# Order and array quarters of the 64x64 products of a chunked recurrence, and the halves of its output bank

## The chip, the cores and the metric

The kernel runs on one core of one Trainium2 chip. The metric is the device time of the whole program in microseconds; 3 runs gave 843.79, 843.86 and 844.13, median 843.86 us. The profile shown is of a further execution, which took 844.05 us.

A core has a matrix engine (TensorE, PE in the profile, its weight loads listed as PEld), a vector engine (DVE), a scalar engine (ACT), GpSimd (POOL) and SyncE (SP), which here issues the loads of the weights. TensorE reads SBUF and writes PSUM; a matmul with 64 contraction rows and 64 output columns uses one quarter of the 128x128 array: its rows are set by the SBUF partitions of its operands (0 to 63 or 64 to 127), its columns by the PSUM partitions of its output. A quarter is called diagonal here when both are the same half, off-diagonal when they are not.

## The reference

One layer of a hybrid decoder on 512 tokens of 1024 channels, in float32: a norm, one input projection, two mixers (sparse attention and RWKV-7), a gated merge with an output projection, and a gated MLP. The change is in the RWKV-7 mixer, whose scan over tokens is, for each of 8 heads with a 64x64 state:

```python
def step(state, inp):
    r_t, w_t, k_t, v_t, a_t, b_t = inp
    sa = jnp.einsum('bhij,bhj->bhi', state, a_t)
    state = state * w_t[:, :, None, :] + sa[..., None] * b_t[:, :, None, :] + v_t[..., None] * k_t[:, :, None, :]
    return state, jnp.einsum('bhij,bhj->bhi', state, r_t)
...
_, y = lax.scan(step, state0, xs)
```

`y` is then normed per head, gated and projected.

## The kernel before

The scan is done in 8 chunks of 64 tokens (`C = 64`, `NCH = 8`). What a chunk needs of its own tokens alone is made beforehand and lies in SBUF: `AR` (decayed a and r vectors), `AB` (masked 64x64 products of a and r with b and k, the inverse of a triangular matrix among them), `BKT` (b and k transposed) and `UV`, of which one half holds the values v and the other half is filled in by the loop. Heads go in 4 pairs p with r = 0 or 1 within the pair; r decides the half of the partitions.

The loop over chunks c (line 935) has, in this order on TensorE, which is given its instructions as the program has them there (`tc.manual_schedule`, line 930):

- X (lines 937 to 941): the state `M0` times a, 8 products of 64x64 added to what `x_own` (lines 922 to 927) left in the same PSUM bank for this chunk. X's products have operands and output in the same half, `x_own`'s read the other half than they write.
- Y's first part (lines 942 to 944): `M0` times r, 8 products into a second bank, operands and output in the same half. In chunk 0 there is no state, and both are left out.
- DVE copies X to `Xs` (line 946); then a piece of other work, see below.
- U (lines 948 to 951): the inverse times `Xs`, 8 products. ACT copies one half of it into `UV` (line 952), DVE the other (line 953). Behind U on TensorE follows `x_own(c + 1)` (line 956), which opens the next chunk's X in another bank; then another piece of other work.
- the state update (lines 959 to 970): `BKT` times `UV` into the bank `Mp`, 8 products of 128 rows and 64 columns, and two operations on DVE that make the next state `M1`. The last chunk has none.
- Y's second part (lines 971 to 974): the r part of `AB` times `UV`, 8 products of 128 rows; two ACT copies take Y to `Ys` (lines 977, 978). Every second chunk `group_norm` norms 128 tokens and gates them (line 854).

X, U and the bank `gg` of `group_norm` share two PSUM banks (`pb()`), Y, `Mp` and others two more (`pa()`).

The other work comes from the generator `fill_chain` (line 880), one step at each `next(fill)`: dense products of the normed input with weight tiles of 128 columns (`dense_fm_g`, line 402: 16 matmuls with a tile's high part, with a pause after 12 of them, and 8 with its low part) and, in the first chunks, the first layer of the compression MLP (`compress`, line 786), which reads its weights as they were loaded. Weights pass through `wload` (line 262: SP issues a load of 512 KB into one of 3 buffers `raw`), and `wsplit_` (line 279: ACT writes the high part `whi`, DVE the rest `wlo`, two buffers each). A buffer `raw` is free again when the split, or TensorE's last product with it, is done. Between the compression's weights k and v and the next dense tile, loads are issued in that order: k, v, tile.

DVE, ACT and SP run what a scheduler put in order; each runs its queue in order.

Of the kernel before, what the change touches and what calls it, by code (L numbers as in the profile page):

```python
# [23 lines left out]
DH = 64  # L24
H = 8
NH2 = H // 2
C = 64
NCH = S // C
# [52 lines left out]
def hybrid_block(ctx: ExitStack, tc: tile.TileContext, A: dict, out: bass.AP):  # L81
# [25 lines left out]
    def bank(tag, bufs, shape=(128, 512)):  # L107
        return ps.tile(list(shape), F32, name="ps_" + tag, tag=tag, bufs=bufs)

    def mmb():  # L110
        return bank("mm", 4)

    def pa():
        return bank("a", 2)

    def pb():
        return bank("b", 2)

    def mm(o, l, r, start, stop):
        te.matmul(o, lhsT=l, rhs=r, start=start, stop=stop)  # L120

    def act(o, i, f=AF.Copy, **kw):
        sc.activation(o, i, f, **kw)  # L123

    def tt(o, a, b, op):
        v.tensor_tensor(o, a, b, op=op)  # L126

    def ts(o, a, s1, s2, op0=ALU.mult, op1=ALU.add):
        if s2 is None:
            v.tensor_scalar(o, a, s1, None, op0=op0)  # L130
        else:
            v.tensor_scalar(o, a, s1, s2, op0=op0, op1=op1)
# [44 lines left out]
    def rstd(ap, n, eps=1e-6, tag=""):  # L177
        p, w = ap.shape
        m, y = (cp.tile([128, 32], F32, name=k, tag=k + tag, bufs=2)[0:p, 0:w] for k in ("rs_m", "rs_y"))
        ts(m, ap, 1.0 / n, eps)  # L180
        ts(ap.bitcast(I32), m.bitcast(I32), -0.5, float(0x5f3759df))
        for i in range(3):
            tt(y, ap, ap, ALU.mult)
            stt(y, y, -0.5, m, ALU.mult, ALU.mult)
            stt(ap, y, 1.5, ap, ALU.add, ALU.mult)
# [209 lines left out]
    def run(g):  # L395
        while True:
            try:
                next(g)
            except StopIteration as e:
                return e.value  # L400
# [23 lines left out]
    AR = mp.tile([128, NH2, NCH, 2, C], F32, name="AR", tag="AR")  # L424

    AB = abp.tile([128, NCH, NH2, 2, 128], F32, name="AB")
    BKT = rp.tile([128, NCH, NH2, 2, DH], F32, name="BKT")
    UV = rp.tile([128, NCH, NH2, 2, DH], F32, name="UV")
# [193 lines left out]
    for g in range(2):  # L622
        for b in range(2):
            r = 64 * g + 32 * b
# [107 lines left out]
    for b in (1, 0):  # L732
        for g in range(2):
            r = 64 * g + 32 * b
# [119 lines left out]
    def group_norm(c0, Ys):  # L854
        n1 = tp.tile([128, H], F32, name="n1", tag="n1", bufs=2)
        bc = n1[:, :, None].to_broadcast([128, H, DH])
        v.tensor_reduce(n1, Ys, axis=AX.X, op=ALU.add)
        ts(n1, n1, -1.0 / DH, None)
        tt(Ys, Ys, bc, ALU.add)
        sq = tp.tile([128, H, DH], F32, name="sq", tag="o", bufs=2)  # L860
        act(sq, Ys, AF.Square)
        v.tensor_reduce(n1, sq, axis=AX.X, op=ALU.add)
        rstd(n1, DH, 64e-5, "g")
        tt(Ys, Ys, bc, ALU.mult)
        yield
        qs = slice(C * c0, C * c0 + 128)
        pt = pa()
        gg = pb()
        o = tp.tile([128, NH2, 128], F32, name="o", tag="o", bufs=2)
        for p in range(NH2):  # L870
            ps_ = slice(128 * p, 128 * p + 128)
            te.transpose(pt[:, ps_], Ys[:, 2 * p:2 * p + 2].rearrange("p h d -> p (h d)"), ident)
            mm(gg[:, ps_], g2[:, ps_], sg[:, qs], True, True)
        for p in range(NH2):
            act(o[:, p], pt[:, 128 * p:128 * p + 128], AF.Identity, scale=col("rwkv_ln_g", p),
                bias=col("rwkv_ln_b", p))
        tt(o, o, BO[:, :, qs], ALU.add)
        tt(BO[:, :, qs], o, gg.rearrange("p (a t) -> p a t", a=NH2), ALU.mult)
# [26 lines left out]
    def bias_rows(a):  # L905
        o = 127 - 16 * a
        nc.sync.dma_start(BT[16 * a:16 * a + 16, :, 256:512],
                          vd[:, 0:16 * 384].rearrange("h (i m) -> i h m", m=384)[:, :, o:o + 256])

    def bias_compressed():  # L910
        nc.gpsimd.memset(BC.rearrange("p j g e n -> p (j g e) n")[:, :, 31:56], NEG)
        for j in range(2):
            src = BT.rearrange("p (g j e) n -> p j g e n", g=2, j=2)[:, j]
            v.tensor_copy(BC[:, j, :, :, 0:15], src[:, :, :, 256:257].to_broadcast([128, 2, 2, 15]))
            v.tensor_copy(BC[:, j, :, :, 15:31], src[:, :, :, 271:512:16])
# [3 lines left out]
    def hsl(r, n=64):  # L919
        return slice(64 * r, 64 * r + n)  # L920

    def x_own(c, X):
        for p in range(NH2):
            for r in range(2):
                o = hsl(1 - r)
                mm(X[hsl(r), 64 * p:64 * p + 64], AB[o, c, p, r, 0:64], UV[o, c, p, r, :], p == 0,
                   c == 0 and p == NH2 - 1)


    with tc.manual_schedule(engines={mybir.EngineType.PE}):  # L930
        M0 = Ys = gn = None
        X = pb()
        x_own(0, X)
        next(fill, None)
        for c in range(NCH):
            Y = pa()
            if M0 is not None:
                for p in range(NH2):
                    for r in range(2):
                        mm(X[hsl(r), 64 * p:64 * p + 64], AR[hsl(r), p, c, 0, :], M0[hsl(r), p, :], False,  # L940
                           p == NH2 - 1)
                for p in range(NH2):
                    for r in range(2):
                        mm(Y[hsl(r), 64 * p:64 * p + 64], AR[hsl(r), p, c, 1, :], M0[hsl(r), p, :], p == 0, False)
            Xs = tp.tile([128, NH2, DH], F32, name="Xs", tag="Xs", bufs=2)
            v.tensor_copy(Xs, X[:, 0:256].rearrange("p (a d) -> p a d", d=DH))
            next(fill, None)
            U = pb()
            for p in range(NH2):
                for r in range(2):  # L950
                    mm(U[hsl(r), 64 * p:64 * p + 64], AB[hsl(r), c, p, r, 0:64], Xs[hsl(r), p], True, True)
            act(UV[0:64, c, :, 0, :], U[0:64, 0:256].rearrange("p (a d) -> p a d", d=DH))
            v.tensor_copy(UV[64:128, c, :, 1, :], U[64:128, 0:256].rearrange("p (a d) -> p a d", d=DH))
            if c < NCH - 1:
                X = pb()
                x_own(c + 1, X)
            next(fill, None)
            if c < NCH - 1:
                Mp = pa()
                for p in range(NH2):  # L960
                    for r in range(2):
                        mm(Mp[hsl(r), 64 * p:64 * p + 64], BKT[:, c, p, r, :], UV[:, c, p, r, :], True, True)
                M1 = tp.tile([128, NH2, DH], F32, name="M", tag="M", bufs=2)
                mpv = Mp[:, 0:256].rearrange("p (a d) -> p a d", d=DH)
                pc = PC[:, :, c:c + 1].to_broadcast([128, NH2, DH])
                if M0 is None:
                    tt(M1, mpv, pc, ALU.mult)
                else:
                    tt(M1, M0, mpv, ALU.add)
                    tt(M1, M1, pc, ALU.mult)  # L970
            for p in range(NH2):
                for r in range(2):
                    mm(Y[hsl(r), 64 * p:64 * p + 64], AB[:, c, p, r, 64:128], UV[:, c, p, r, :],
                       M0 is None and p == 0, p == NH2 - 1)
            if c % 2 == 0:
                Ys = tp.tile([128, H, DH], F32, name="Ys", tag="Ys", bufs=2)
            for r in range(2):
                act(Ys[hsl(c % 2), r::2, :], Y[hsl(r), 0:256].rearrange("p (h d) -> p h d", d=DH))
            if c % 2 == 1:
                gn = group_norm(c - 1, Ys)  # L980
                if c < NCH - 1:
                    next(gn)
            M0 = M1
            if 4 <= c < 6:
                for a in range(4 * c - 16, 4 * c - 12):
                    bias_rows(a)
            if c == NCH - 2:
                bias_compressed()
            if c == NCH - 1:
                for h0 in range(0, H, 4):  # L990
                    act(BT[:, h0:h0 + 4, 0:256], BT[:, h0:h0 + 4, 256:257].to_broadcast([128, 4, 256]))
            next(fill, None)
            if gn is not None and c % 2 == 0:
                run(gn)
                gn = None
# [294 lines left out]
    with tc.manual_schedule(engines=KTS):  # L1290
        for t in range(NT):
            qs = slice(128 * t, 128 * t + 128)
            p = mmb()
# [88 lines left out]
```

## Time and profile before

| | |
|---|---|
| median of the runs | 843.86 us |
| profiled execution | 844.05 us, span 842.3 us |
| TensorE busy | 829.1 us of the span |
| DVE, ACT, POOL busy | 514.0, 405.9, 52.4 us |
| stretch of the recurrence | from 180 to 285 us of the span |

The granted TensorE clock is 1.000 over the span. A row of the timeline has the start in us from the span's beginning, the time in us, engine, source line, operation, what is written and read, the shape and how many instructions were merged into the row; in brackets the idle time before it and what ended that. Line 120 is the helper `mm`, 123 `act`, 126 `tt`, 135 `stt`; which work a row is, is told by the tiles.

### The profile page before, as it was taken

To read this page: it belongs to the slowest core of one execution; us is meant where nothing else is said; L and a number is where in the kernel's file an instruction comes from. 1 tells how busy PE (TensorE), PEld (TensorE's weight loads), DVE (VectorE), ACT (ScalarE), POOL (GpSimd) and SP (SyncE) were. 2 spreads that over 40 slices of the span, in tenths; PEclk is the share of its full clock that TensorE was granted. 3 is DMA by queue.
4 is the path that set the end of the run, shared out by engine and by line. 5 is a ranking of instruction groups with operands and counts; after the bars stand their busy time and mean duration, and the time that the engine had idled before them with its cause. 6 is when DMAs were issued, how large, how long until landed. Compare 5 with 4: busy or idle time off the path is not lost.

```text
span 842.3 us, 12845 instructions
## 1 busy us (share of the span) xinstructions
PE 829.1 (98%) x5097; PEld 674.3 (80%) x5097; DVE 514.0 (61%) x998; ACT 405.9 (48%) x784; POOL 52.4 (6%) x69
## 2 busy tenths in 40 slices
PE   7999999999999999999999999999999999999998
PEld 6777778887787886777788988888888888888886
DVE  5477779963556678888675576666556666322222
ACT  6766655452545677677344454444444444221210
POOL 6200020140000110111000000000000000000000
PEclk9999999999999999999999999999999999999999
DMA  7432222335461320010167033333333332223421
GB/s 228 115 82 68 75 75 76 92 104 156 126 126 51 88 63 13 22 31 26 51 204 234 0 99 90 90 97 100 100 100 100 96 90 93 98 100 113 138 75 51
DMA packets 109104, 78.73 MB, mean 93 GB/s; under 512 B 3869, under 2 KB 97748, under 8 KB 109044
## 3 DMA queue, kind: packets, MB, share of 16 engines
q1 hardware_dynamic: 106512, 73.51, 30.0%
q0 software_dynamic: 1472, 1.86, 1.0%
q10 hardware_dynamic: 1060, 2.55, 1.0%
q8 instruction: 40, 0.66, 0.3%
q14 instruction: 20, 0.16, 0.1%
HBM read 74.56 MB, written 2.29 MB: 91 GB/s over the span
## 4 chain that ended last, share of the span: by engine, by line
PE 53%; DVE 0%; DVEq 0%; issue 0%
PE ps_mm L120 52%; PE ps_b L203 0%; PE ps_a L203 0%; PE ps_a L120 0%; PE ps_b L1186 0%; PE ps_mm L1186 0%; DVE x L126 0%; DVEq L1378 0%; PE ps_a L1138 0%
## 5 line engine op out<-in xcount | busy, mean ns | idle before, releaser
L296 DVE TENSOR_TENSOR wlo<-raw,whi 128x1024 fp32r<-128x1024 f32 (+1 forms) x111 | 131.5, 1186 | 187.2 <-PE ps_mm L120 158.8
L120 PE MATMUL ps_mm<-hh,whi 128*128 128x512 f32 (+1 forms) x624 | 242.6, 391 | 0.0
L120 PE MATMUL ps_mm<-hl,whi 128*128 128x512 f32 (+1 forms) x624 | 240.4, 387 | 0.0
L123 ACT ACTIVATE whi<-raw 128x1024 fp32r<-128x1024 f32 (+3 forms) x124 | 123.3, 996 | 171.1 <-PE ps_mm L120 143.0
L120 PE MATMUL ps_mm<-hh,wlo 128*128 128x512 f32 (+1 forms) x624 | 151.8, 384 | 0.0
L120 PEld LDWEIGHTS ps_mm<-hh,whi 128*128 128x128 f32 x624 | 117.3, 188 | 26.7 <-issue 1.3
L120 PEld LDWEIGHTS ps_mm<-hl,whi 128*128 128x128 f32 x624 | 117.4, 188 | 23.5 <-issue 1.0
L120 PEld LDWEIGHTS ps_mm<-hh,wlo 128*128 128x128 f32 x624 | 115.1, 188 | 23.4
L120 PE MATMUL ps_mm<-whi,aT 128*128 128x512 f32 x352 | 84.5, 390 | 0.0
L120 PEld LDWEIGHTS ps_mm<-whi,aT 128*128 128x128 f32 x352 | 65.9, 188 | 14.3 <-issue 0.4
L135 DVE SCALAR_TENSOR_TENSOR cgv<-ps_mm,cw,cgv 128x511 f32<-128x511 f32 (+1 forms) x88 | 65.4, 746 | 1.6
L123 ACT ACTIVATE cgv<-ps_mm,cw 128x512 f32<-128x512 f32 x44 | 34.3, 781 | 23.3 <-PE ps_mm L120 23.3
L120 PE MATMUL ps_mm<-wlo,aT 128*128 128x512 f32 x176 | 44.3, 389 | 0.0
L123 ACT ACTIVATE P<-P,nm 128x512 f32<-128x512 f32 (+3 forms) x64 | 35.4, 553 | 14.9 <-DVE nm L1160 14.9
L123 ACT ACTIVATE aT<-cgv 128x512 fp32r<-128x512 f32 x22 | 13.9, 632 | 56.8 <-DVE cgv L126 56.8
L120 PEld LDWEIGHTS ps_mm<-wlo,aT 128*128 128x128 f32 x176 | 33.0, 188 | 6.9
L123 ACT ACTIVATE cgv<-cgv 128x512 f32<-128x512 f32 x22 | 13.9, 632 | 41.0 <-DVE cgv L135 41.0
L296 POOL TENSOR_TENSOR wlo<-raw,whi 128x512 fp32r<-128x512 f32 (+3 forms) x13 | 20.4, 1569 | 203.9 <-PE ps_mm L120 148.1
L1160 DVE CUSTOM_DVE_ANT_0 P<-ps_a,AB 128x512 f32<-128x512 f32 (+3 forms) x64 | 29.4, 484 | 4.2 <-PE ps_a L120 3.7
L126 DVE TENSOR_TENSOR x<-x,ps_mm 128x512 f32<-128x512 f32 (+1 forms) x17 | 11.0, 654 | 22.6 <-PE ps_mm L120 20.2
L126 DVE TENSOR_TENSOR aT<-cgv,aT 128x512 fp32r<-128x512 f32 x22 | 15.2, 693 | 14.7 <-ACT aT L123 14.7
L120 PE MATMUL ps_a<-KH,qst 128*128 128x512 f32 (+3 forms) x64 | 21.3, 348 | 1.5 <-DVE nm L1160 0.9
(356 smaller groups left out, 1201.7 us busy)
## 6 DMA issues: line engine op xcount, KB each, us to landing
raw<-in_w_up_dram SPq DMA_DIRECT2D x44, 512.0 KB, 3.8
raw<-in_w_in_dram SPq DMA_DIRECT2D x38, 512.0 KB, 3.9
raw<-in_w_down_dram SPq DMA_DIRECT2D x22, 512.0 KB, 3.6
raw<-in_w_out_dram SPq DMA_DIRECT2D x8, 512.0 KB, 3.9
xt<-in_x_dram SPq DMA_DIRECT2D x4, 512.0 KB, 5.8
raw<-in_cmp_w_k_dram SPq DMA_DIRECT2D x4, 512.0 KB, 4.4
raw<-in_cmp_w_v_dram SPq DMA_DIRECT2D x4, 512.0 KB, 4.4
raw<-in_w_proj_b_dram SPq DMA_DIRECT2D x8, 256.0 KB, 2.7
```

What stands on the lines that cost most here:

```text
L120: te.matmul(o, lhsT=l, rhs=r, start=start, stop=stop)
L123: sc.activation(o, i, f, **kw)
L126: v.tensor_tensor(o, a, b, op=op)
L135: v.scalar_tensor_tensor(o, a, s, b, op0=op0, op1=op1)
L296: eng.tensor_tensor(lo, raw, hi.bitcast(F32), op=ALU.subtract)
L1160: v.tensor_tensor_reduce(out=P[:, i], in0=sp[:, N * (i - i0):N * (i - i0) + N], in1=BT[:, h, 384 - 128 * qt:512], scale=-1.0, scalar=-NEG, ...
```

## The change

In the four places that the diff shows:

- Y's first part is moved into X's loop over head pairs: two products of X, two of Y, and so on; Y's outputs go to the other half of the bank (`hsl(1 - r)`), and so does Y's second part. The ACT copies to `Ys` read the exchanged halves, so that `Ys` holds what it held.
- `x_own` takes the head pairs as an argument. The next chunk's bank X is opened before U, and U's loop does two products of U and two of `x_own(c + 1)` in turn.

The number, shapes and operands of the products stay. On DVE, POOL and SP the order of the instructions and what they wait for is the same as before; on ACT the copy of U into `UV` stands one place later in four chunks: behind a copy to `vt` in chunk 0, and behind a tanh of 128x512 in chunks 1, 3 and 5.

```diff
@@ -919,12 +919,13 @@
     def hsl(r, n=64):
         return slice(64 * r, 64 * r + n)
 
-    def x_own(c, X):
-        for p in range(NH2):
+    def x_own(c, X, ps_=range(NH2)):
+        for p in ps_:
             for r in range(2):
                 o = hsl(1 - r)
                 mm(X[hsl(r), 64 * p:64 * p + 64], AB[o, c, p, r, 0:64], UV[o, c, p, r, :], p == 0,
                    c == 0 and p == NH2 - 1)
+
 
 
     with tc.manual_schedule(engines={mybir.EngineType.PE}):
@@ -939,21 +940,21 @@
                     for r in range(2):
                         mm(X[hsl(r), 64 * p:64 * p + 64], AR[hsl(r), p, c, 0, :], M0[hsl(r), p, :], False,
                            p == NH2 - 1)
-                for p in range(NH2):
                     for r in range(2):
-                        mm(Y[hsl(r), 64 * p:64 * p + 64], AR[hsl(r), p, c, 1, :], M0[hsl(r), p, :], p == 0, False)
+                        mm(Y[hsl(1 - r), 64 * p:64 * p + 64], AR[hsl(r), p, c, 1, :], M0[hsl(r), p, :], p == 0, False)
             Xs = tp.tile([128, NH2, DH], F32, name="Xs", tag="Xs", bufs=2)
             v.tensor_copy(Xs, X[:, 0:256].rearrange("p (a d) -> p a d", d=DH))
             next(fill, None)
             U = pb()
+            if c < NCH - 1:
+                X = pb()
             for p in range(NH2):
                 for r in range(2):
                     mm(U[hsl(r), 64 * p:64 * p + 64], AB[hsl(r), c, p, r, 0:64], Xs[hsl(r), p], True, True)
+                if c < NCH - 1:
+                    x_own(c + 1, X, (p,))
             act(UV[0:64, c, :, 0, :], U[0:64, 0:256].rearrange("p (a d) -> p a d", d=DH))
             v.tensor_copy(UV[64:128, c, :, 1, :], U[64:128, 0:256].rearrange("p (a d) -> p a d", d=DH))
-            if c < NCH - 1:
-                X = pb()
-                x_own(c + 1, X)
             next(fill, None)
             if c < NCH - 1:
                 Mp = pa()
@@ -970,12 +971,12 @@
                     tt(M1, M1, pc, ALU.mult)
             for p in range(NH2):
                 for r in range(2):
-                    mm(Y[hsl(r), 64 * p:64 * p + 64], AB[:, c, p, r, 64:128], UV[:, c, p, r, :],
+                    mm(Y[hsl(1 - r), 64 * p:64 * p + 64], AB[:, c, p, r, 64:128], UV[:, c, p, r, :],
                        M0 is None and p == 0, p == NH2 - 1)
             if c % 2 == 0:
                 Ys = tp.tile([128, H, DH], F32, name="Ys", tag="Ys", bufs=2)
             for r in range(2):
-                act(Ys[hsl(c % 2), r::2, :], Y[hsl(r), 0:256].rearrange("p (h d) -> p h d", d=DH))
+                act(Ys[hsl(c % 2), r::2, :], Y[hsl(1 - r), 0:256].rearrange("p (h d) -> p h d", d=DH))
             if c % 2 == 1:
                 gn = group_norm(c - 1, Ys)
                 if c < NCH - 1:
```

## The prediction

> **What bounds the kernel now.** I read the page first: its span, the busy shares and the chain of work that ended last. The profiled execution took 844.05 us, 842.3 us of it span; the runs shown have a median of 843.86 us, 0.19 us below it.
>
> ```profile
> span 842.3 us, 12845 instructions
> PE 829.1 (98%) x5097; PEld 674.3 (80%) x5097; DVE 514.0 (61%) x998; ACT 405.9 (48%) x784; POOL 52.4 (6%) x69
> PE 53%; DVE 0%; DVEq 0%; issue 0%
> ```
>
> TensorE is busy 98% of the span, and all that the chain names is TensorE. So time taken out of its stream shortens the kernel, unless something that does not depend on TensorE holds the stream up again behind the place of the saving. I therefore read, second, the order of time on TensorE through one chunk of the recurrence, to price the blocks that are edited, and third, the timelines of SP, ACT and DVE around the places where TensorE needs their results, to see whether the saving survives.
>
> **What the edited blocks cost now.** This is chunk c = 1 on TensorE, with the single block of the last chunk (c = 7) below it. A product is one call of `mm` and leaves two matmul records, so 8 products are x16. Columns: start, duration, instructions, count.
>
> ```profile
> 195.91 0.68 PE L120 MATMUL ps_b<-M,AR 64*64 64x64 f32 x16
> 196.42 0.63 PE L120 MATMUL ps_a<-M,AR 64*64 64x64 f32 x16
> 196.98 0.50 PE L120 MATMUL ps_mm<-hh,whi 128*128 128x512 f32 x1
> ...
> 199.93 0.51 PE L120 MATMUL ps_b<-Xs,AB 64*64 64x64 f32 x10
> 200.23 0.27 PE L120 MATMUL ps_b<-UV,AB 64*64 64x64 f32 x2
> 200.27 0.28 PE L120 MATMUL ps_b<-Xs,AB 64*64 64x64 f32 x3
> ...
> 200.40 0.51 PE L120 MATMUL ps_b<-UV,AB 64*64 64x64 f32 x11
> 200.84 0.44 PE L120 MATMUL ps_mm<-raw,sg 128*64 128x256 f32 x2
> ```
>
> ```profile
> 280.94 0.68 PE L120 MATMUL ps_b<-Xs,AB 64*64 64x64 f32 x16
> 281.55 0.50 PE L120 MATMUL ps_mm<-hh,whi 128*128 128x512 f32 x1
> ```
>
> I count a block from its first start to the first start of what follows, since ends are modelled. One set of 8 products alone takes 281.55 - 280.94 = 0.61 us. X and Y (both on the diagonal quarters) take 196.98 - 195.91 = 1.07 us: the second set adds 0.46 us, so the two sets run one behind the other. U (diagonal) and the next chunk's X part from `x_own` (off-diagonal) take 200.84 - 199.93 = 0.91 us, and here the rows show something: two UV matmuls start at 200.23, after 10 of the 16 Xs matmuls, and the other Xs ones start behind and among them. So matmuls of different quarters already run side by side wherever both are near the head of the stream, and the second set adds only 0.30 us.
>
> **The change part by part.**
>
> *Interleaving X with Y, seven blocks (c = 1 to 7).* Y's outputs move to the other half, so its products use the off-diagonal quarters, and come pair by pair between X's. No matmul is added or removed. If the four quarters run as side by side as they do from 200.23 on, the block costs what one set costs, 0.61 us, plus a little for two more starts in the first step; I take 0.62. Gain: 1.07 - 0.62 = 0.45 us a block. Bounds: no gain (0) if the quarters take turns, and 0.46 at best.
>
> *Interleaving U with x_own, seven blocks (c = 0 to 6).* By the same step 0.91 - 0.62 = 0.29 us a block. Bounds: 0.30 at best; at worst the overlap that exists is lost and the block becomes 1.07 us like X and Y today, -0.16 us.
>
> [...]
>
> *Y's last products and the copy to Ys.* Same count, same shapes, the two column halves in the other order. The state update Mp before them ends on the half where Y now begins; at most one step of the alternation is lost there, (0.46 us / 8 steps) = 0.06 us a chunk, at best nothing. I take 0, because several instructions ahead are looked at, as the 200.23 row shows.
>
> *Waits.* Y's and x_own's first products now stand before the end of X and U; each waits for its bank, and behind it are queued the rest of X or U and with them the next chunk. The latest reader of such a bank that I found is group_norm's product on DVE in chunk 3 (5 and 7 alike):
>
> ```profile
> 227.43 0.69 DVE L126 TENSOR_TENSOR BO<-o,ps_b 128x512 f32<-128x512 f32 x1
> ...
> 229.31 0.51 PE L120 MATMUL ps_b<-Xs,AB 64*64 64x64 f32 x10
> ```
>
> It ends at 228.12, 1.19 us before U starts, and X with Y takes at most 0.46 of that: cost 0; without that cover it would be the 0.29 of this block. ACT's copy of U into UV moves behind one more activation in chunks 0, 1, 3 and 5; DVE's copy of the other half, behind a weight split, is the later one today, so I take 0 there as well.
>
> Sum on TensorE alone: 7 x 0.45 + 7 x 0.29 = 5.2 us. **That is not what arrives at the end**, because in chunks 0 to 2 TensorE runs just ahead of a chain that starts before the first edited block and does not wait for it. Rows of SP, then ACT, then DVE, then TensorE:
>
> ```profile
> 185.48 0.46 SPq L267 DMA_DIRECT2D raw<-in_w_in_dram  x1
> 192.97 0.37 SPq L267 DMA_DIRECT2D raw<-in_cmp_w_k_dram  x1
> ...
> 202.68 0.37 SPq L267 DMA_DIRECT2D raw<-in_cmp_w_k_dram  x1
> ...
> 212.65 0.37 SPq L267 DMA_DIRECT2D raw<-in_w_in_dram  x1
> ```
>
> ```profile
> 200.34 1.06 ACT L123 ACTIVATE whi<-raw 128x1024 fp32r<-128x1024 f32 x1 [6.91 <-DMA raw<-in_w_in_dram]
> ...
> 210.30 1.06 ACT L123 ACTIVATE whi<-raw 128x1024 fp32r<-128x1024 f32 x1 [2.68 <-DMA raw<-in_w_in_dram]
> ...
> 216.76 1.06 ACT L123 ACTIVATE whi<-raw 128x1024 fp32r<-128x1024 f32 x1 [3.32 <-DMA raw<-in_w_in_dram]
> ```
>
> ```profile
> 211.39 1.22 DVE L296 TENSOR_TENSOR wlo<-raw,whi 128x1024 fp32r<-128x1024 f32 x1 [2.12 <-ACT whi L123]
> ...
> 217.85 1.23 DVE L296 TENSOR_TENSOR wlo<-raw,whi 128x1024 fp32r<-128x1024 f32 x1 [1.08 <-ACT whi L123]
> 219.00 0.41 DVE L135 SCALAR_TENSOR_TENSOR QK<-QK,ps_mm 128x256 f32<-128x256 f32 x1
> 219.44 0.43 DVE L953 COPY UV<-ps_b 64x256 f32<-64x256 f32 x1
> ```
>
> ```profile
> 219.46 1.09 PE L120 MATMUL ps_a<-UV,BKT 128*64 128x64 f32 x15
> ...
> 221.00 0.50 PE L120 MATMUL ps_mm<-hh,whi 128*128 128x512 f32 x1
> ```
>
> Read it backward. The state update of chunk 2 (219.46) needs DVE's copy of UV, done at 219.44 + 0.43 = 219.87. That copy stands behind the split of a weight tile (217.85), which follows ACT's half of the split (216.76), which waited for the tile's DMA, issued at 212.65, 0.04 us after the split at 211.39 ended and freed a buffer; that one follows ACT's at 210.30, which again waited for a DMA, of the group issued from 202.68 on, and so back, in steps of about 9.8 us (202.68 - 192.97, 212.65 - 202.68), to the load issued at 185.48, which is before chunk 0's U, the first block that the change shortens. From there to 219.87 the chain is DMA, ACT split, DVE split, next issue, and waits for no edited block. TensorE already waits at its end: 221.00 - 219.46 = 1.54 us for a pair of sets that adds up to about 1.07 (X and Y above have as many matmuls), so about 0.46 us.
>
> What comes earlier in chunks 0 to 2 is therefore given back there: 3 x 0.29 + 2 x 0.45 = 1.77 us more wait, and the dense product at 221.00 stays at 221.00. A part of that wait may fall on the weight tile of 210.30, if TensorE comes to it before it is split; the place of the loss is then another, the sum is not.
>
> From chunk 3 on, the timeline shows the splits on ACT and DVE waiting for TensorE's matmuls and no longer for DMAs, so they move with TensorE. The narrowest place I found is chunk 4:
>
> ```profile
> 244.56 0.43 DVE L953 COPY UV<-ps_b 64x256 f32<-64x256 f32 x1
> ...
> 246.12 0.69 PE L120 MATMUL ps_a<-UV,BKT 128*64 128x64 f32 x16
> ```
>
> There 246.12 - 244.99 = 1.13 us are left, and the two blocks of the chunk take 0.74 of them even if DVE does not move at all. So the gain that stays is 5 x 0.45 (X with Y, c = 3 to 7) + 4 x 0.29 (U with x_own, c = 3 to 6) = 3.4 us. Profiled: 844.05 - 3.4 = 840.65; against the median of the runs, 843.86 - 3.4 = **840.5 us**.
>
> **The rivals.**
>
> *All of it arrives: 838.7 us.* If the load chain of chunks 0 to 2 gets earlier with TensorE, 843.86 - 5.2. For it: two of the three loads of each group go into buffers that TensorE frees. Against it: the first of each group is issued just behind DVE's split (211.39 + 1.22 = 212.61, issue 212.65), and the others stand behind it in SP's queue.
>
> *Half a gain: 843.1 us.* The overlap may need the look-ahead that it has now and get no better by a finer order: every block then costs 0.91. X and Y gain 0.16 five times, U and x_own nothing: 843.86 - 0.8. For it: the second set only began to overlap after 10 of 16 matmuls. Against it: in the new order the four quarters lie within one pair of the head, closer than the six that were passed at 200.23.
>
> *The quarters take turns, slower: 844.5 us.* If TensorE keeps two matmuls side by side and the next in program order must start first, each block needs 16 steps, 1.07 us. X and Y stay as they are, U and x_own lose 0.16 each; the first three are covered by the 0.46 us wait of chunk 2 (0.48, so 0.02 is left), the other four cost 0.64. Place: U's block from chunk 3 on; it decides as soon as such a block takes over 0.91 us. For it: X and Y today stand one behind the other. Against it: they share quarters today, and the 200.23 row.
>
> **How the numbers follow.** Chances: 0.62 for the forecast, 0.12 for all of it, 0.10 for half, 0.12 for turns, 0.04 for anything else, such as a full drain of the array at each change of quarters, which would cost more than turns. The forecast's own range is 839.9 to 841.1 (blocks of 0.61 to 0.70 us). The range that is to hold 8 in 10 goes from the rival below to the one of half a gain: 838.5 to 843.1 us. A run tells 0.2%, 1.7 us, from no change. Faster than 842.2 are the forecast, all of it and the better part of half: 0.77. Within 0.2% are the rest of half and turns: 0.19. Slower: 0.04.
>
> **What the changed profile would show.** X with Y, and U with x_own, each take 0.6 to 0.65 us from first start to the next dense product, in all chunks. The copies of UV in chunk 2 on DVE stand where they are, near 219.4, and TensorE idles nearly 2 us before them, an idle that the waits view names with DVE's UV copy. The dense product behind it starts near 221.0, as before. From there each chunk is 0.74 us shorter, and the first attention work comes 3.4 us earlier. I am wrong about the blocks if they take 0.9 us or more, about the chain if the 221.0 product comes before 220.5, and about the rest if a wait opens behind chunk 3.

## The result, and the profile after

The changed kernel takes 841.14 us (median of 6 runs, 840.65 to 841.47), the kernel before, beside it, 843.87 us (6 runs, 843.79 to 844.13): ratio 0.9966, 95% interval 0.9956 to 0.9976. So it is faster by 2.7 us; forecast were 840.5 us, a gain of 3.4.

The profiled execution took 841.33 us, 839.5 us of it span, against 844.05 and 842.3. The first lines of the page and its chain:

```profile
span 839.5 us, 12845 instructions
PE 824.8 (98%) x5097; PEld 669.9 (80%) x5097; DVE 514.1 (61%) x998; ACT 405.4 (48%) x784; POOL 52.4 (6%) x69
PE 53%; DVE 0%; DVEq 0%; issue 0%
```

The same number of instructions, the same 98%: TensorE's busy time falls by 4.3 us (829.1 to 824.8), the span by 2.8. The difference is idle time on TensorE that was not there before. The timeline finds both parts. First the X with Y block of chunk 1, on PE (start, duration, instructions, count):

```profile
195.82 0.27 PE L120 MATMUL ps_b<-M,AR 64*64 64x64 f32 x2
195.84 0.27 PE L120 MATMUL ps_a<-M,AR 64*64 64x64 f32 x2
195.93 0.23 PE L120 MATMUL ps_b<-M,AR 64*64 64x64 f32 x2
195.94 0.23 PE L120 MATMUL ps_a<-M,AR 64*64 64x64 f32 x2
...
196.29 0.23 PE L120 MATMUL ps_a<-M,AR 64*64 64x64 f32 x2
196.45 0.50 PE L120 MATMUL ps_mm<-hh,whi 128*128 128x512 f32 x1
```

Two X matmuls (ps_b) and two Y matmuls (ps_a), one in each quarter, start within 0.02 us of each other; the second four start 0.11 us behind the first, and every further four 0.06 us behind the last. The block takes 196.45 - 195.82 = 0.63 us instead of 1.07. U with x_own looks the same:

```profile
199.40 0.27 PE L120 MATMUL ps_b<-Xs,AB 64*64 64x64 f32 x2
199.41 0.27 PE L120 MATMUL ps_b<-UV,AB 64*64 64x64 f32 x2
...
200.02 0.65 PE L120 MATMUL ps_mm<-raw,sg 128*64 128x256 f32 x4
```

0.62 us instead of 0.91. All fourteen edited blocks take 0.62 to 0.63.

Now chunk 2, from its X to the dense product behind its state update, after (in the prediction's rows that product started at 221.00). In brackets stands the idle time before the group and what ended it:

```profile
208.88 0.27 PE L120 MATMUL ps_b<-M,AR 64*64 64x64 f32 x2
...
212.36 0.50 PE L120 MATMUL ps_mm<-hh,whi 128*128 128x512 f32 x1 [0.69 <-ACT whi L123]
...
215.30 0.27 PE L120 MATMUL ps_b<-Xs,AB 64*64 64x64 f32 x2
...
219.12 0.33 PE L120 MATMUL ps_a<-UV,BKT 128*64 128x64 f32 x2 [0.18 <-ACT UV L123]
220.60 0.62 PE L120 MATMUL ps_a<-UV,BKT 128*64 128x64 f32 x13 [1.15 <-DVE UV L957]
...
221.68 0.50 PE L120 MATMUL ps_mm<-hh,whi 128*128 128x512 f32 x1
```

and the same places in the kernel before:

```profile
209.69 0.27 PE L120 MATMUL ps_b<-M,AR 64*64 64x64 f32 x2
...
215.59 0.33 PE L120 MATMUL ps_b<-Xs,AB 64*64 64x64 f32 x3
```

X comes 209.69 - 208.88 = 0.81 us earlier, but U only 0.29, although X with Y is 0.45 shorter: 0.81 + 0.45 - 0.29 = 0.97 us went into waits, most of it (0.69) for a weight tile that ACT had not yet split. From U to the dense product it is 6.38 us instead of 221.00 - 215.59 = 5.41, although U with x_own is 0.29 shorter: 1.26 us more, this time for the copies of UV. What TensorE waits for, on ACT and on DVE:

```profile
211.25 1.06 ACT L123 ACTIVATE whi<-raw 128x1024 fp32r<-128x1024 f32 x1 [4.42 <-DMA raw<-in_w_in_dram]
...
217.44 1.06 ACT L123 ACTIVATE whi<-raw 128x1024 fp32r<-128x1024 f32 x1 [3.19 <-DMA raw<-in_w_in_dram]
```

```profile
212.34 1.23 DVE L296 TENSOR_TENSOR wlo<-raw,whi 128x1024 fp32r<-128x1024 f32 x1 [3.86 <-ACT whi L123]
...
218.53 1.23 DVE L296 TENSOR_TENSOR wlo<-raw,whi 128x1024 fp32r<-128x1024 f32 x1 [0.82 <-ACT whi L123]
219.68 0.41 DVE L135 SCALAR_TENSOR_TENSOR QK<-QK,ps_mm 128x256 f32<-128x256 f32 x1
220.12 0.43 DVE L957 COPY UV<-ps_b 64x256 f32<-64x256 f32 x1
```

It is the chain of the prediction, load, split on ACT, split on DVE, copy of UV, but the copy starts at 220.12, not at 219.44, and the product behind the update at 221.68, not at 221.00. From there on the gain is kept. The last products of Y in chunk 7, after and before:

```profile
281.72 0.69 PE L120 MATMUL ps_a<-UV,AB 128*64 128x64 f32 x16
```

```profile
284.50 0.69 PE L120 MATMUL ps_a<-UV,AB 128*64 128x64 f32 x16
```

From 221.68 to 281.72 are 60.04 us; before, from 221.00 to 284.50, 63.50. That is 3.46 us gained; 0.68 lost at 221.68; and 557.8 us from there to the end of the span in both. 3.46 - 0.68 = 2.78, the 2.8 us of the spans.

### The profile page after: what moved, and what is told of

The parts are those of the page before. It is cut to its first block, busy times and chain, and to the rows that moved or that the text cites. A ratio compares the mean times of both kernels' runs of the same rounds, so it can differ in the third digit from the quotient of the medians.

```text
span 839.5 us, 12845 instructions
## 1 busy us (share of the span) xinstructions
PE 824.8 (98%) x5097; PEld 669.9 (80%) x5097; DVE 514.1 (61%) x998; ACT 405.4 (48%) x784; POOL 52.4 (6%) x69
## 4 chain that ended last, share of the span: by engine, by line
PE 53%; DVE 0%; DVEq 0%; issue 0%
PE ps_mm L120 52%; PE ps_b L203 0%; PE ps_a L203 0%; PE ps_a L120 0%; PE ps_b L1187 0%; PE ps_mm L1187 0%; DVE x L126 0%; DVEq L1379 0%; PE ps_a L1139 0%
```

## The experiments

Each kernel's profile was read at the same places. "Block" is the time from first start to the next first start; "product" is the start of the dense product behind chunk 2's state update; "stretch" is from there to Y's last products of chunk 7. All in us. The ratio is to the kernel before, timed beside it.

| kernel | X with Y | U with x_own | product | stretch | span | median (runs) | ratio, 95% interval |
|---|---|---|---|---|---|---|---|
| before | 1.07 | 0.91 | 221.00 | 63.50 | 842.3 | 843.87 (6) | |
| changed | 0.62 | 0.62 | 221.68 | 60.04 | 839.5 | 841.14 (6) | 0.9966, 0.9956 to 0.9976 |
| again | 0.62 | 0.62 | 221.70 | 60.09 | 839.5 | 841.27 (5) | 0.9965, 0.9953 to 0.9978 |
| half_only | 0.91 | 0.91 | 221.51 | 62.68 | 841.9 | 843.61 (11) | 0.9992, 0.9983 to 1.0001 |
| order_only | 1.08 | 0.91 | 221.61 | 63.51 | 842.8 | 844.26 (11) | 1.0001, 0.9992 to 1.001 |
| xy_only | 0.62 | 0.91 | 221.01 | 61.23 | 840.0 | 841.91 (9) | 0.9976, 0.9966 to 0.9985 |
| u_only | 1.08 | 0.62 | 221.46 | 62.31 | 841.5 | 843.78 (11) | 0.9999, 0.999 to 1.0007 |
| k2_own | 0.62 | 0.62 | 220.57 | 60.08 | 838.4 | 840.15 (5) | 0.9954, 0.9941 to 0.9966 |
| k2_own_before | 1.08 | 0.91 | 220.79 | 63.50 | 842.0 | 843.71 (11) | 0.9998, 0.9989 to 1.0007 |
| uv2_act | 0.62 | 0.62 | 220.24 | 60.06 | 838.0 | 840.05 (5) | 0.9955, 0.9943 to 0.9968 |
| pool4 | 0.62 | 0.62 | 221.10 | 60.04 | 838.9 | 840.56 (5) | 0.9956, 0.9944 to 0.9969 |
| no_chain | 0.62 | 0.62 | 221.67 | 61.26 | 840.6 | 842.43 (7) | 0.9974, 0.9963 to 0.9985 |
| no_chain_before | 1.08 | 0.91 | 221.51 | 63.49 | 842.7 | 844.56 (11) | 1.0004, 0.9996 to 1.0013 |
| u_only_no_chain | 1.08 | 0.62 | 222.91 | 63.16 | 843.8 | 843.71 (11) | 0.9995, 0.9987 to 1.0004 |

The kernel before had a median of 844.16 us beside again, half_only, order_only and xy_only, 843.86 beside u_only, k2_own, k2_own_before and uv2_act, and 844.20 beside the other four. The spans and columns are those of the profiled execution, which is one of the runs; of u_only it is the second fastest (843.27 us), of u_only_no_chain the slowest (845.55).

### The blocks: halves, order, and each part alone

**half_only.** The kernel before, with only Y's bank turned round:

```diff
-                        mm(Y[hsl(r), 64 * p:64 * p + 64], AR[hsl(r), p, c, 1, :], M0[hsl(r), p, :], p == 0, False)
+                        mm(Y[hsl(1 - r), 64 * p:64 * p + 64], AR[hsl(r), p, c, 1, :], M0[hsl(r), p, :], p == 0, False)
...
-                    mm(Y[hsl(r), 64 * p:64 * p + 64], AB[:, c, p, r, 64:128], UV[:, c, p, r, :],
+                    mm(Y[hsl(1 - r), 64 * p:64 * p + 64], AB[:, c, p, r, 64:128], UV[:, c, p, r, :],
...
-                act(Ys[hsl(c % 2), r::2, :], Y[hsl(r), 0:256].rearrange("p (h d) -> p h d", d=DH))
+                act(Ys[hsl(c % 2), r::2, :], Y[hsl(1 - r), 0:256].rearrange("p (h d) -> p h d", d=DH))
```

> Only Y's outputs go to the other half; the order stays X then Y, and U then x_own. Theory (look-ahead of TensorE passes a few matmuls, so the overlap is partial as in U with x_own before): X with Y takes about 0.91 us instead of 1.07, U with x_own stays at 0.91, five blocks from chunk 3 on give 5 x 0.16 = 0.8 us: 843.1. Rival 1 (other quarters suffice, any order): X with Y 0.62, gain 2.25, 841.6. Rival 2 (without the finer order there is no overlap): 1.07, 843.9.

Measured: blocks of 0.91, a stretch 63.50 - 62.68 = 0.82 us shorter, where 0.8 was expected; its median is 0.55 below that of before (844.16), an interval that just reaches no change; in its profile 0.51 of the 0.82 is lost at the product. X with Y of chunk 1 on PE:

```profile
196.05 0.51 PE L120 MATMUL ps_b<-M,AR 64*64 64x64 f32 x10
196.35 0.27 PE L120 MATMUL ps_a<-M,AR 64*64 64x64 f32 x2
196.39 0.28 PE L120 MATMUL ps_b<-M,AR 64*64 64x64 f32 x3
...
196.52 0.51 PE L120 MATMUL ps_a<-M,AR 64*64 64x64 f32 x11
196.96 0.50 PE L120 MATMUL ps_mm<-hh,whi 128*128 128x512 f32 x1
```

These are the rows of U with x_own before: after 10 matmuls of X the first two of Y pass the other six. The look-ahead exists, is short, and gives 0.16 us a block; the finer order gives the other 0.29.

**order_only.** The kernel before, with only the loop header between X and Y taken out, so that they alternate on the same two quarters:

```diff
                         mm(X[hsl(r), 64 * p:64 * p + 64], AR[hsl(r), p, c, 0, :], M0[hsl(r), p, :], False,
                            p == NH2 - 1)
-                for p in range(NH2):
                     for r in range(2):
                         mm(Y[hsl(r), 64 * p:64 * p + 64], AR[hsl(r), p, c, 1, :], M0[hsl(r), p, :], p == 0, False)
```

> Only the order of X and Y is interleaved; Y stays on the diagonal quarters, U and x_own stay one behind the other. Theory (two sets on the same two quarters run one behind the other in any order): X with Y 1.07 us, no gain, 843.9. Rival (the order alone hides weight loads): under 1.0 us, 843.3 or less.

Measured: 1.08 us a block, stretch 63.51. On PE:

```profile
196.21 0.33 PE L120 MATMUL ps_b<-M,AR 64*64 64x64 f32 x4
196.38 0.28 PE L120 MATMUL ps_a<-M,AR 64*64 64x64 f32 x4
196.50 0.28 PE L120 MATMUL ps_b<-M,AR 64*64 64x64 f32 x4
```

X and Y take turns, four records (one product in each of the two quarters) every 0.12 us. Order without other quarters is worth nothing, other quarters without order a third of the gain: the change needs both.

**xy_only** and **u_only** take one half of the change each: the first has the edits to X, Y and Ys, the second those to U and x_own.

> X with Y changed in full (other half and interleaved), U and x_own as before. Theory: X with Y 0.62 us in all chunks, U with x_own 0.91; what comes up to chunk 2 is given back at the load chain, five blocks from chunk 3 on give 5 x 0.45 = 2.25 us: 841.6, plus or minus what the load chain varies (0.7). Rival (all of it arrives): 7 x 0.45 = 3.15, 840.7.

> Only U and x_own are interleaved; X and Y as before. Theory: U with x_own 0.62 us in chunks 0 to 6, X with Y 1.07; chunks 0 to 2 are given back at the load chain, four blocks give 4 x 0.29 = 1.16 us: 842.7, plus or minus what the load chain varies (0.7). Rival (all of it arrives): 7 x 0.29 = 2.0, 841.8.

Measured in the stretch: 63.50 - 61.23 = 2.27 us for xy_only (2.25 expected) and 63.50 - 62.31 = 1.19 for u_only (1.16 expected); together 3.46, what the whole change shows. The median of xy_only, 841.91, is 2.25 us below the 844.16 of the kernel before beside it, as the theory has it, and 1.2 off the rival. That of u_only, 843.78, misses: its profiled execution took 843.27, but its 11 runs lie between 842.60 and 845.27, most of them near before's. Its profile shows the product 0.46 us late, which leaves 0.7 of the 1.19; why the other runs lose more was not profiled and stays open (the slowest, 845.27, has a mean clock of 0.998, the others 0.999 or 1.000). So the timed runs of u_only alone show no gain from U with x_own; beside xy_only in the same round, the whole change (again, 841.27) shows 0.64 us more than xy_only.

### The chain in front of chunk 2

**again** is the changed kernel once more.

> The changed kernel once more, for the spread of the load chain. Theory A (the third group of loads, first issue to last landing, is longer in the changed kernel for good, 8.55 us against 7.54 before): the new profile again shows 8.3 us or more, the dense product behind chunk 2's state update starts about 41.3 us after the load whose issue was at 185.68, as it did (221.68 - 185.68 = 36.0 to that product), and the median stays at 841.1. Theory B (the length of that group varies from run to run): the new profile shows another length, anywhere from 7.0 to 8.6 us, and the span follows it one to one where the group is last.

Neither theory holds as written. The third group of loads, from first issue to the end of its DVE split (the DVE rows of both kernels have the same 1.23 us split), starts at 202.83 and ends at 213.37, 10.54 us, against 213.57 - 202.61 = 10.96 in the first profile of the changed kernel and 212.61 - 202.68 = 9.93 before; so it does vary. (To the start of ACT's split, the row nearest to the landing of which the expectation speaks, it is 8.22, 8.64 and 7.62.) But the product stands at 221.70 as the first time, and the runs at 841.13 to 841.46 are as close together as those of before.

The kernels above give more readings of the chain, since they leave the loads alone. From the issue that stood at 185.48 before to the product it took 35.52 us before, 36.00 and 36.02 in the changed kernel, 35.84 in half_only, 35.78 in order_only, 35.32 in xy_only and 35.86 in u_only. order_only saves nothing on TensorE and is 0.26 longer than before; xy_only saves 0.9 us there and is 0.20 shorter. So the chain has no fixed length: it varies by 0.7 us between profiles, and its length does not follow what TensorE saves. In the first profile of the changed kernel the extra lies in that third group, which is 1.03 us longer than before, while the parts of the chain ahead of it (202.61 - 185.68 = 16.93 instead of 17.20) and behind it (221.68 - 213.57 = 8.11 instead of 8.39) are shorter. ACT waits for the load there (the row at 211.25); why the load takes longer stays open. Whether the two readings of the changed kernel are high by chance, seven profiles don't tell.

**k2_own** and **k2_own_before** loosen the chain at its front, in the changed kernel and in the one before: one of the eight compression tiles goes to a buffer of its own.

```diff
-                        yield A["cmp_w1_" + s_][0][512 * s4:512 * s4 + 512], 4, 256, None
+                        yield A["cmp_w1_" + s_][0][512 * s4:512 * s4 + 512], 4, 256, "k2" if (s4, s_) == (2, "k") else None
...
-            raw = wp.tile([128, kt, n], F32, name="raw", tag="raw", bufs=3)
+            if eng == "k2":
+                raw, eng = sg0[:, 2:4].rearrange("p m (a n) -> p (m a) n", n=n), None
+            else:
+                raw = wp.tile([128, kt, n], F32, name="raw", tag="raw", bufs=3)
```

> The changed kernel, with the third compression tile of k (the one loaded at 193.16) in a buffer of its own (the unused upper half of sg0) instead of one of the three raw buffers, so that it is loaded much earlier and the two loads behind it move up. Theory (the chain from load to load holds the dense product behind chunk 2's state update at 221.68): the second and third group of loads land 2 us or more earlier, TensorE no longer waits in chunk 2, and what chunks 0 to 2 save (1.77 us) and what the chain cost on top (0.68) arrive, 841.1 - 2.4 = 838.7; if a part of the chain remains, between 838.7 and 840.3. Rival (TensorE is held there by its own order or by the copies of UV on DVE): 841.1, unchanged.

> The kernel before, with the same buffer for the third compression tile of k. Theory (before, TensorE waits only about 0.46 us for the load chain, and the rest of the chunks not at all): gain of 0.3 to 0.7 us, 843.2 to 843.6. Rival (the earlier loads are worth the same to both kernels, so that they are a gain of their own): 2.4 us, 841.5.

The same edit is worth 841.14 - 840.15 = 1.0 us to the changed kernel and 843.86 - 843.71 = 0.15 to the one before, a little less than the 0.3 expected. It is no gain of its own: it frees what the change had saved. Of the 2.4 us expected 1.0 came, inside the 838.7 to 840.3 given for a chain of which a part remains. Splits on ACT in k2_own:

```profile
208.38 1.06 ACT L123 ACTIVATE whi<-raw 128x1024 fp32r<-128x1024 f32 x1 [7.10 <-DMA raw<-in_w_in_dram]
214.72 1.06 ACT L123 ACTIVATE whi<-raw 128x1024 fp32r<-128x1024 f32 x1 [1.25 <-DMA raw<-in_w_in_dram]
```

They come 2.9 and 2.7 us earlier than at 211.25 and 217.44, and the wait for the tile is gone. What is left is the wait for UV, first for ACT's copy, then for DVE's, on PE:

```profile
218.61 0.33 PE L120 MATMUL ps_a<-UV,BKT 128*64 128x64 f32 x2 [0.61 <-ACT UV L123]
219.49 0.62 PE L120 MATMUL ps_a<-UV,BKT 128*64 128x64 f32 x13 [0.55 <-DVE UV L960]
```

**uv2_act** loosens the other end: chunk 2's second copy of UV goes to ACT.

```diff
-            v.tensor_copy(UV[64:128, c, :, 1, :], U[64:128, 0:256].rearrange("p (a d) -> p a d", d=DH))
+            (act if c == 2 else v.tensor_copy)(UV[64:128, c, :, 1, :], U[64:128, 0:256].rearrange("p (a d) -> p a d", d=DH))
```

> The changed kernel, with chunk 2's copy of the lower half of UV on ACT instead of DVE, where it stands behind a weight split. Theory (in chunk 2, TensorE waits for that copy, ended at about 220.5, and ACT is free from 218.5 on): the copy is done by 219.5, the dense product behind the state update starts about 1.0 us earlier, at 220.7, and 840.1. Rival (something else, such as the next weight tile, ends within 0.3 us of the copy): 840.8 to 841.1.

Measured 840.05 us (839.83 to 840.36, all below the changed kernel's fastest run). ACT makes both copies, 218.34 to 219.10, and the update no longer breaks off behind its first two matmuls:

```profile
218.76 1.02 PE L120 MATMUL ps_a<-UV,BKT 128*64 128x64 f32 x15 [0.35 <-ACT UV L123]
...
220.24 0.50 PE L120 MATMUL ps_mm<-hh,whi 128*128 128x512 f32 x1
```

**pool4, no_chain, no_chain_before, u_only_no_chain.** Another way to free DVE there: the weight split in front of the copy goes to POOL. pool4 is the changed kernel with that alone; the other three have it beside k2_own's buffer, in the changed kernel, in the one before, and in u_only.

```diff
-            yield cols(w_in, O_GA + 128 * m)
+            yield cols(w_in, O_GA + 128 * m, eng=pool_ if m == 4 else v)
```

> The changed kernel with only the second loosening: the split in front of chunk 2's copy of UV on POOL instead of DVE, no buffer added. Theory: DVE's copy is done by about 219.4, the wait for the third weight tile at 211 to 212.4 stays, the dense product behind the state update starts 1.1 to 1.3 us earlier than 221.67, and the time is 840.0, as with the copy on ACT.

> The changed kernel with both ends of the chain loosened: the third compression tile of k in a buffer of its own, as in k2_own, and the split of the weight tile in front of chunk 2's copy of UV on POOL instead of DVE (1.23 us off DVE at that place). Theory (all 5.2 us are saved on TensorE, and only this chain held a part back): DVE's copy of UV is done by about 218.0, the state update of chunk 2 starts without a wait at about 217.9 and takes 1.08 us, the dense product behind it starts at about 219.0 instead of 221.67, and the time is 841.2 - 2.65 = 838.5. Rival (a further supply limits chunk 2 as soon as this one is gone): 839.5 to 840.1, as with each loosening alone.

> The same two loosenings in the kernel before. Theory (before, TensorE did not wait there any more once the third tile of k had its own buffer: its state update of chunk 2 took 1.08 us): as that kernel, 843.7, and the distance to the changed kernel with the same loosenings is 7 x 0.45 + 7 x 0.29 = 5.2 us. Rival (the loosening is a gain of its own, not of the change): 842.5 or less, distance 4 us or less.

> Only U and x_own interleaved, with the same two loosenings. Theory (the interleaving of U with x_own is worth 0.29 us in each of 7 chunks, and was lost in the load chain where it was tried alone): 7 x 0.29 = 2.0 us against the kernel before with the loosenings: 841.7. Rival (interleaving U with x_own gives nothing outside the blocks' own rows, as the timed runs of it alone suggest): 843.7.

pool4 gains half of what was expected at the product (221.10 instead of 221.68, not 220.5), with a median of 840.56. With the split gone from DVE, the operation in front of its copy of UV waits 1.24 us for ACT, which splits the same tile first (DVE's row at 219.09 in the last section); so the copy starts at 219.54, only 0.58 earlier. The other three missed: no_chain is 2.3 us slower than k2_own, no_chain_before 0.85 slower than k2_own_before (the kernel before was 0.34 slower beside them), the distance between the two is 2.1 us instead of 5.2, and u_only_no_chain has its product as late as 222.91. So they don't test what they were made for; that the median of u_only_no_chain, 843.71, is the number of its rival tells nothing either. DVE, POOL and ACT of no_chain show why:

```profile
215.99 2.30 DVE L132 TENSOR_SCALAR QK<-QK 128x256 f32<-128x256 f32 x1 [0.55 <-ACT QK L123]
...
218.40 0.42 DVE L126 TENSOR_TENSOR QK<-QK,ps_mm 128x256 f32<-128x256 f32 x1
...
219.78 0.43 DVE L960 COPY UV<-ps_b 64x256 f32<-64x256 f32 x1
```

```profile
215.76 2.38 POOL L299 TENSOR_TENSOR wlo<-raw,whi 128x1024 fp32r<-128x1024 f32 x1 [18.73 <-ACT whi L123]
```

```profile
218.85 0.42 ACT L123 ACTIVATE QK<-QK 128x256 f32<-128x256 f32 x1 [2.89 <-DVE QK L126]
219.17 0.36 ACT L123 ACTIVATE UV<-ps_b 64x256 f32<-64x256 f32 x1
```

The split takes 2.38 us on POOL, and DVE's first operation during it, which takes 0.28 us in k2_own, ends 0.15 us behind it, after 2.30. ACT's next operation needs what DVE makes behind that one, and ACT's copy of UV stands behind ACT's operation: it starts at 219.17 instead of 218.20 in k2_own, and DVE's copy at 219.78 instead of 219.01. TensorE, done with its dense products earlier, stands for 1.74 us on end, for ACT's copy, and in the window behind that its granted clock is 0.61 instead of 1.00. PE of no_chain, and its windows (busy time of each engine with its count, granted clock, DMA share, GB/s):

```profile
219.59 0.33 PE L120 MATMUL ps_a<-UV,BKT 128*64 128x64 f32 x2 [1.74 <-ACT UV L123]
```

```profile
216.00:220.00 4.00, 2.18 (x11) 1.38 (x9) 3.94 (x6) 1.15 (x3) 2.14 (x1) 1.00 0.52 120
220.00:224.00 4.00, 3.74 (x36) 3.14 (x37) 2.28 (x4) 2.35 (x5) 0.00 (x0) 0.61 0.60 158
```

Its stretch is 61.26 instead of 60.04 although its blocks take 0.62 us: the 1.2 us are those of the lower clock. In the profile of u_only_no_chain TensorE stands for 1.59 us there (from 218 to 222 us it is idle for 1.91 in all), the granted clock is 0.92 in that window and 0.66 from 222 to 226 us, and the stretch is 63.16 instead of 62.31. So the whole 5.2 us was not seen to arrive in any run, and whether it would with every wait gone is open. The nearest to it is the pair of k2_own kernels: their spans differ by 842.0 - 838.4 = 3.6 us, and k2_own still shows a wait of 0.61 us in front of its update and one of 0.55 in it, the update with Y's last products taking 220.57 - 218.61 = 1.96 us; k2_own_before shows none there, with an update of 1.08:

```profile
219.71 0.69 PE L120 MATMUL ps_a<-UV,BKT 128*64 128x64 f32 x16
220.23 0.64 PE L120 MATMUL ps_a<-UV,AB 128*64 128x64 f32 x16
220.79 0.50 PE L120 MATMUL ps_mm<-hh,whi 128*128 128x512 f32 x1
```

0.61 us before the update and 1.96 - 1.08 = 0.88 in it make 1.5; 3.6 + 1.5 = 5.1. That is a sum over two profiles, not a run.

## Why the prediction was right, and where it was off

**The blocks: right.** 0.62 us for each of the fourteen, as taken, hence 0.45 and 0.29 a block. half_only and order_only show that it is for the reason given (four quarters at once, if all four are at the head of the order), and not for the order or the other half alone. The rival of half a gain described what half_only does. The rival in which the quarters take turns does not hold here: products that share rows of the array start 0.01 to 0.02 us apart, and so do their weight loads (195.82 and 195.84 on PEld in X with Y of chunk 1); and in half_only Y's first matmuls start at 196.35, before X's last ones at 196.39.

**What stays behind chunk 2: right.** 5 x 0.45 + 4 x 0.29 = 3.4 us were predicted, 3.46 measured, and the parts alone add up to it. No wait opened in that stretch, so the edits costed at nothing there (the other half order of Y's last products, the bank waits, ACT's copy one place later) cost nothing.

**What is given back in chunks 0 to 2: right in kind, too small in size.** The prediction let the product stay at 221.00 and the UV copy at 219.4; they stand at 221.68 and 220.12. The new waits in chunk 2 are 0.97 + 1.26 = 2.23 us: the 1.77 that was saved, and 0.46 more. Of the 0.68 at the product, 0.20 were there before the first edited block (chunk 0's first products start at 180.30 in the profile of before and at 180.50 after; order_only has 180.65), and 0.48 came from the chain. The failing step is the one that took the chain's length from one profile as fixed: 35.52 us there, 35.3 to 36.0 in seven. With 36.0 and the later start the forecast would have been 3.4 - 0.7 = 2.7 us, which is what was measured. That the measured 841.14 ends within 0.04 us of the forecast's own range (839.9 to 841.1) is luck: that range was made for blocks of up to 0.70 us and had no term for the chain. That part of the wait falls on the weight tile split from 210.30 on was said, and 0.69 us of it do.

**All of it arrives: did not.** That the chain is what stops it is shown by k2_own and uv2_act, which touch nothing but the chain and bring 1.0 and 1.1 us, while the same buffer brings 0.15 before. (uv2_act's edit was not run in the kernel before; by the prediction's rows at most about 0.46 us of wait was left there for it to remove.)

## What to carry to other kernels

Here two sets of 8 products of 64x64 in different quarters of the array took 0.62 us where the program alternates between the quarters, little more than one set alone (0.61); one set behind the other they took 0.91, a third of the gain from 1.07. When a stage on the busiest engine gets shorter, look for the chain of loads and splits that begins ahead of it: what is saved before its end is lost there, and its length from one profile carries an error, here up to 0.7 us, a quarter of the gain. When such a chain is the limit, move its late end off the engine it queues on, as uv2_act does with one line, or give it a buffer, and price the engine that gets the work: POOL's split won 0.58 us at the product in pool4, and in no_chain it cost more than DVE's queue had (the product at 221.67, 220.57 in k2_own).

## What the runs showed of the hardware

**Beside POOL's split of a weight tile, operations of DVE between SBUF tiles took 2.30 and 2.27 us instead of 0.28 and 0.17.** In no_chain DVE's operation that reads and writes SBUF, 0.28 us in k2_own, runs from 215.99 to 218.29, POOL's split from 215.76 to 218.14. In no_chain_before POOL's split runs from 215.48 to 217.86, and DVE's next operation, one of a row of 0.17 us each, ends at 217.87:

```profile
215.60 2.27 DVE L135 SCALAR_TENSOR_TENSOR n<-rs_y,n 128x8 f32<-128x8 f32 x1
```

In pool4 operations that read PSUM took 0.42 and 0.43 us in the middle of a split (218.83 to 221.19), as in the changed kernel (0.41 and 0.43):

```profile
219.09 0.42 DVE L135 SCALAR_TENSOR_TENSOR QK<-QK,ps_mm 128x256 f32<-128x256 f32 x1 [1.24 <-ACT QK L123]
219.54 0.43 DVE L957 COPY UV<-ps_b 64x256 f32<-64x256 f32 x1
220.63 1.64 DVE L296 TENSOR_TENSOR wlo<-raw,whi 128x1024 fp32r<-128x1024 f32 x1 [0.67 <-ACT whi L123]
```

The next split on DVE, with its operands in SBUF, took 1.64 us instead of 1.23, 0.41 more; POOL's split had 0.56 us left when it started. The rows of 2.30 and 2.27 us end 0.15 and 0.01 us behind POOL's split; the split in pool4 lost 0.15 us less than POOL's still had to run. The kernel before has such a row too, and others that are not longer: beside POOL's split of 128x560 (177.24 to 178.61) a DVE operation of 128x8 took 1.36 us (177.28 to 178.64), those around it 0.16 to 0.19; beside POOL's split from 124.19 to 126.58 a transpose on DVE between SBUF tiles took 2.01 to 2.05 us, as the ones behind it. What tells the two kinds apart was not shown.

**Behind waits of 1.74 and 1.59 us the granted clock was 0.61 and 0.66.** In no_chain the dense products behind the wait of 1.74 us start 0.42 us apart, against 0.23 at a granted clock of 1.00 (before, 221.34 to 221.57); from 221.67 the six steps to 224.36 take 2.69 us, against 1.50 in the kernel before (221.00 to 222.50):

```profile
222.27 0.63 PE L120 MATMUL ps_mm<-hl,whi 128*128 128x512 f32 x1
222.69 0.63 PE L120 MATMUL ps_mm<-hh,whi 128*128 128x512 f32 x1
```

They lie in the window with the granted clock of 0.61, and the difference is the 1.2 us by which the stretch is longer. The two fastest of its 7 runs, 840.41 and 841.15 us, had a mean clock of 1.000, the other five, 842.35 to 842.96, one of 0.998. In the changed kernel, with waits of 0.18 and 1.15 us at the same place, the clock stayed at 1.00, and in xy_only, with one of 0.84, as well. Of the fourteen profiles only those of no_chain and u_only_no_chain have a mean clock below 0.999 (0.998 and 0.997). At the start of the span TensorE waits for 4.9 us in the kernel before and for 5.1 in the changed one, and from 4 to 8 us its clock is 1.00. So it was not shown that the length of a single wait decides, nor at what length.
